# Three more odd up steps of two FFNs made as seven products, the first down tiles prepared in the last pair, and four smaller edits

## The chip, the cores and the metric

One core of a Trainium2 chip runs the whole program. The metric is the device time of one execution in microseconds (us). The engines are those of the profile: PE (TensorE matmul), PEld (its weight loads), DVE (VectorE), ACT (ScalarE), POOL (GpSimd), SP (SyncE, which here only issues transfers). A product of fp32 matrices is made in three passes of fp32r matmuls: each operand is split into a high half (a copy rounded to fp32r, made by ACT) and a low half (the rest, made by DVE), and high x high, low x high and high x low are added up in one PSUM bank.

## The reference, cut to what matters

A trunk of two layers on 512 tokens of width 1024. Layer 0 mixes by gated linear attention, layer 1 by a sparse attention (NSA) over keys and values shared from the state between the layers; both also attend to a memory. Behind each mixer comes the same kind of FFN, which is where most of the change lies:

```python
def conv_ffn(x, w_up, conv_w, conv_b, w_down):
    S = x.shape[1]
    u = x @ w_up                                  # 512 x 1024 @ 1024 x 5632
    u_pad = jnp.pad(u, ((0, 0), (CONV_WIDTH - 1, 0), (0, 0)))
    hc = conv_b
    for j in range(CONV_WIDTH):                   # width 3, along the tokens
        hc = hc + conv_w[j] * u_pad[:, j:j + S]
    a, b = split_cols(hc, (FFN_DIM, FFN_DIM))     # FFN_DIM 2816
    return (jax.nn.silu(a) * b) @ w_down          # 2816 x 1024

for i in range(2):
    ...
    h = h + concatenate([main, mem_attention]) @ w_out[i]
    h = h + conv_ffn(rmsnorm(h, norm_ffn[i]), w_up[i], conv_w[i], conv_b[i], w_down[i])
return rmsnorm(h, final_norm)
```

One edit lies in the compression of the shared keys and values (`silu(flat @ cmp_w1 + b1) @ cmp_w2 + b2`), right behind which layer 1 projects its queries.

## The kernel before

**The up steps.** The 2816 columns of a and of b are cut into NJ = 22 steps of 128; step j makes columns 128j to 128j+127 of a (half 0) and of b (half 1), features on the partitions and the 512 tokens along a row. A *plain* step (the loop at the end of `up`, L1268) is 2 x 24 matmuls of 512 columns: 8 slices of the 1024 input features, 3 passes each. `wget` loads a weight tile of 128 x 1024 on SP's queue and splits it. `gate` then makes silu(a) * b.

**Pairs.** For the odd steps listed in `FAST`, 9 to 19 in layer 0 and 7 to 19 in layer 1, the function `pairs` does an even step and the odd one behind it together. The even one is plain (`plain`, L1162, 48 matmuls of 512 columns). The odd one is a product of 2 x 2 blocks (a and b; first and last 512 input features; first and last 256 tokens) and is made by Strassen's scheme as seven products in place of eight (`product`, L1168): 7 x 4 slices x 3 passes = 84 matmuls of 256 columns. Products 1 to 3 use plain blocks of x, products 4 to 7 use sums of blocks of x. `forms` makes these sums in place of the rows x was made from and splits them: the high halves into one tile of tag "h" (the buffer of the residual h, which has been spilled to DRAM; a tile takes 128 x (V_N + 7 + 4096) floats), the low halves into scratch of the FFN. In the plain part of `up` two calls of `forms` stand behind steps fast[0]-3 and fast[0]-2, the third in the first pair.

Within `pairs`, `load` issues the next transfers four items ahead, `high` and `low` split a tile, `step` does the convolution, `close` and `finish` end the odd step's b in the pair behind it, and the order on ACT and DVE is that of the text (`Ordered`, whose recording line is L201, links each instruction to the one before while `on` is set). At the end of a pair it makes the next pair's first three weights (w0, w1, wa).

**Sums of weights.** The seven products also need sums of blocks of w_up (one block for each fast step) and of w_down (one for each p = 0..10, in both layers). They are formed ahead in DRAM, in the tensor qsum: two copies of 512 KB a block on SP's queue (`copy`, L280, 70 in all), then three accumulating transfers on POOL's queue, of 512, 256 and 256 KB (`pace`, L289, 105 in all; blocks go in groups of three, all first stages of a group ahead of its second). Calls of `copy` and `pace` are spread over the kernel, each behind an instruction that it follows.

**The down product.** It is made from seven products as well. Three of them (5, 7, 6) run inside the up stage: `mms(p, (6,))` and `mms(p, (5, 7))`, where `fill(j, half)` says so in a plain step, or at fixed places in a pair; `weights(p)` loads and splits their weights. Products 1 to 4 run behind the up stage, over tiles of w_down streamed in: `parts(s)` loads and splits tile s, `step(s)` uses it. So L1346 (layer 0, `ffn_features`) and L1535 (layer 1, `ffn_seven`) occur within the up stage and behind it. `back` reloads h from its spill, for the additions of the down product.

**The first query weight.** `project(0)` of layer 1 calls `wget` with a gain: POOL multiplies the raw tile by the gain of the norm (L350), then it is split (L353 ACT, L354 DVE). At that time DVE finishes the compression (`done`, L1982: hid, from which TensorE makes L1933).

In a span of 1222 us the stages lie so: input projections and attention of layer 0 to 208, w_out to 236, up 236 to 514, down to 580; layer 1's mixer 580 to 833, w_out to 872, up 872 to 1148, down and the last norm to 1214.

Of the kernel before, what the change touches and what calls it, by code (L numbers as in the profile page):

```python
# [24 lines left out]
FAST = ((9, 11, 13, 15, 17, 19), (7, 9, 11, 13, 15, 17, 19))  # L25
# [185 lines left out]
class Trunk:  # L211
# [113 lines left out]
    def wget(self, i, gain=None, ks=range(KC), halves=False):  # L325

        nc = self.nc
        raw = self.wload(i)
        if gain is not None and len(ks) <= 4:
            wh = self.t(self.wsp, [128, 1024], "wh", FR)  # L330
            wl = self.t(self.wsp, [128, 1024], "wl", FR)
            n = 1024 // len(ks)
            for r, k in enumerate(ks):
                o = slice(n * r, n * r + n)
                self.split_to(wh[:, o], wl[:, o], raw[:, o], self.gain(gain, k))
                if i == self.W["nsav"][3] and self.mem_scale:
                    self.after(self.high_ins, self.mem_scale)
            return wh, wl
        if gain is not None:
            a, n = V_GAIN + 8 * gain + ks[0], len(ks)  # L340
            g = self.vec[:, a:a + n].unsqueeze(2).to_broadcast([128, n, 1024 // n])
            v = raw.rearrange("p (k c) -> p k c", k=n)
            if halves:
                wh, wl = (self.t(self.wsp, [128, 1024], t, FR) for t in ("wh", "wl"))
                for r in range(2):
                    c, o = slice(n // 2 * r, n // 2 * r + n // 2), slice(512 * r, 512 * r + 512)
                    nc.gpsimd.tensor_tensor(out=v[:, c], in0=v[:, c], in1=g[:, c], op=ALU.mult)
                    self.split_to(wh[:, o], wl[:, o], raw[:, o])
                return wh, wl
            nc.gpsimd.tensor_tensor(out=v, in0=v, in1=g, op=ALU.mult)  # L350
        wh = self.t(self.wsp, [128, 1024], "wh", FR)
        wl = self.t(self.wsp, [128, 1024], "wl", FR)
        self.split_ins = nc.scalar.activation(wh, raw, AF.Copy)  # L353
        self.low_ins = nc.vector.tensor_tensor(out=wl, in0=raw, in1=wh.bitcast(F32), op=ALU.subtract)  # L354
        return wh, wl
# [278 lines left out]
    def gla_layer(self):  # L634
        nc, I, tc = self.nc, self.I, self.tc
        with ExitStack() as outer:
# [30 lines left out]
            with tc.tile_pool(name="glap", bufs=1) as pp:  # L667
# [42 lines left out]
                def queries_keys(i):  # L710
                    j, r = divmod(i, 2)
                    if i < 3:
                        qp = qps[i]
                    else:
                        qp = self.ps("sc" if i == 3 else "acc")
                        self.projA(qp, self.wget(self.W[("glak", "glaq")[r]][j]))
                        if i > 3:
                            self.copy(self.move)
# [73 lines left out]
            with tc.tile_pool(name="glac", bufs=2) as cp:  # L792
# [167 lines left out]
                for P in range(8):  # L960
# [12 lines left out]
                    self.pace(laid[0], 2)  # L973
# [96 lines left out]
    def up(self, l, pool, rows, us, fill, gate, pe, space=None, seven=None):  # L1070
# [12 lines left out]
        def forms(n):  # L1083
# [3 lines left out]
            def halves(q, raw, los):  # L1087
                n = (5, 7, 4, 6).index(q)
                hi = T["high"][:, 1024 * n:1024 * n + 1024].rearrange("p (k t) -> p k t", k=4)
# [25 lines left out]
        def pairs(js):  # L1115
# [8 lines left out]
            for j in js:  # L1124
                p, b = self.downb(l, j // 2 - 1), self.upb(l, j + 1)
                items += [(q(qs, p, 2),), (q(qs, b, 2), q(qs, b, 1)), (q(qd, b, 3), q(qs, b, 3)), (q(qs, p, 0, 2),), (q(qd, b, 0),),
                          (wp[up[2 * j + 4]],), (wp[up[2 * j + 5]],), (wp[up[2 * j + 6]],) if j == js[-1] else first(j + 2)]
# [42 lines left out]
            def step(j, half, u, dst, *parts):  # L1170
                self.conv(l, j, half, u, dst, parts)
                if "act" in parts:
                    self.pace(self.conv_ins, int(l or half or j % 2) + l * half * (j % 2))
                    if l == 0 and half:
                        self.copy(self.conv_ins)
# [17 lines left out]
            for j in js:  # L1193
# [36 lines left out]
                w0 = low(high())  # L1230
                w1 = high()
                dve.tensor_tensor(out=v2, in0=v2, in1=bass.AP(tensor=B.tensor, offset=B.offset + 256, ap=[B.ap[0], [-256, 2], [1, 256]]), op=ALU.subtract)
                w1 = low(w1)
# [3 lines left out]
                mms(p, (5, 7))  # L1237
# [3 lines left out]
                wa = high()  # L1241
                step(j + 1, 0, A, hc[0], "dve")
                act.activation(hc[0], hc[0], AF.Silu)
                wa = low(wa)
# [5 lines left out]
            ready.extend((w0, w1, wa))  # L1250
# [9 lines left out]
        for j in range(NJ):  # L1260
# [9 lines left out]
            if fast and fast[0] - 1 <= j <= fast[-1]:  # L1270
                if j in fast:
                    continue
                if j == fast[0] - 1:
                    pairs(range(j, fast[-1], 2))
                    if l == 0:
                        back(nc.gpsimd)
# [34 lines left out]
            self.pace(self.conv_ins, 3 if l else 1 + j % 2)  # L1311
            if l or j % 2:
                self.copy(self.conv_ins)
# [8 lines left out]
        if l:  # L1322
            back(nc.sync)

    def ffn_features(self, l):
# [42 lines left out]
        with ExitStack() as stack:  # L1368
# [54 lines left out]
            def fill(j, half):  # L1423
                p = j // 2 - 1
                if j == NJ - 1:
                    if half:
                        mms(p, (6,))
                        weights(T - 1)
# [15 lines left out]
            self.up(l, pool, rows, [us[:, half] for half in range(2)], fill, gate, pe, ap, (ops, mms))  # L1444
# [26 lines left out]
            parts(0)  # L1471
            parts(1)
# [42 lines left out]
    def ffn_seven(self, l):  # L1515
# [110 lines left out]
        def end(mms):  # L1626
# [8 lines left out]
            parts(0)  # L1635
            parts(1)
# [85 lines left out]
        with ExitStack() as stack:  # L1722
# [7 lines left out]
            with tc.tile_pool(name=f"up{l}", bufs=2) as pool:  # L1730
# [38 lines left out]
                def fill(j, half):  # L1769
                    p = j // 2 - 1  # L1770
                    if j == NJ - 1:
                        if half:
                            mms(p, (6,))
                            weights(T - 1)
# [17 lines left out]
                self.up(l, pool, rows, u, fill, gate, pe, ap, (ops, mms))  # L1792
# [21 lines left out]
    def nsa_layer(self):  # L1814
        nc, I, tc = self.nc, self.I, self.tc
        GKV, GMIX = 6, 1
        with ExitStack() as outer:
# [194 lines left out]
            def project(a):  # L2012

                wh, wl = self.wget(self.W["nsaq"][a], GMIX)
                if a > 1:
                    after(self.split_ins, self.mem_exp if a == 2 else turned[2 * a - 6])
                ps = self.ps("acc")
# [258 lines left out]
```

## Time and profile before

| | us |
|---|---|
| median of 3 runs (1224.05 to 1224.95) | 1224.61 |
| the profiled execution | 1224.07 |
| its span | 1222.3 |
| mean granted TensorE clock in it | 0.997 |

Busy time by stage, from the view of windows (stretch; its length and then the busy time and instructions of PE, PEld, DVE, ACT, POOL; granted clock, share of DMA, GB/s):

```profile
116.00:208.00 92.00, 92.00 (x897) 79.17 (x896) 72.06 (x226) 50.23 (x151) 33.58 (x60) 1.00 0.84 162
236.00:515.00 279.00, 278.91 (x1652) 248.32 (x1650) 229.24 (x342) 150.64 (x228) 28.82 (x36) 1.00 0.79 211
580.00:833.00 253.00, 249.76 (x1811) 213.53 (x1811) 187.32 (x456) 161.73 (x428) 99.33 (x115) 0.99 0.49 148
872.00:1148.00 276.00, 275.87 (x1502) 239.93 (x1501) 233.63 (x348) 150.44 (x213) 38.36 (x46) 1.00 0.85 204
1148.00:1214.00 66.00, 66.00 (x314) 54.86 (x313) 48.43 (x70) 35.63 (x57) 0.71 (x1) 1.00 0.46 148
```

The second and fourth row are the two up stages. PE is busy in nearly all of each, DVE for 229 of 279 us and 234 of 276. In the group views a row names line, engine, operation, output and inputs with their shapes and a count; a row of instructions begins with its start and its duration; rows in brackets say how long the engine was idle before and what ended that.

### The profile page before, as it was taken

How to read it: one execution, taken by the hardware profiler on the slowest of the kernel's cores; microseconds unless marked ns; L12 is line 12 of the kernel's file. 1: busy time of each engine (PE TensorE's matmuls, PEld its weight loads, DVE VectorE, ACT ScalarE, POOL GpSimd, SP SyncE). 2: the span in 40 equal slices, each digit the busy share in tenths (PEclk: the TensorE clock that was granted, in tenths of full speed). 3: DMA queues.
4: the chain of work that ended last, by engine and by line, in shares of the span. 5: the costliest groups of instructions: out<-in, count | busy, mean ns of one | idle time of the engine just before them, and what ended most of it. 6: DMA issues, size and time to landing. Idle time of an engine off the chain costs nothing.

```text
span 1222.3 us, 20705 instructions
## 1 busy us (share of the span) xinstructions
PE 1211.1 (99%) x7657; PEld 1052.1 (86%) x7657; DVE 950.4 (78%) x1723; ACT 694.0 (57%) x1321; POOL 220.8 (18%) x286
## 2 busy tenths in 40 slices
PE   9999999999999999999999999999999999999997
PEld 7888889888899999899888888888888889988886
DVE  7875887599678888778767577984699888888685
ACT  7656555456445555546534777783456455556454
POOL 1011342010010101100112155662021211110000
PEclk9999999999999999999999999999999999999999
DMA  8587699756779798887765334536799999985544
GB/s 294 187 224 198 143 173 173 272 155 170 181 204 229 212 224 228 254 260 223 213 197 168 84 110 143 180 120 156 235 177 187 242 209 212 216 230 172 173 128 147
DMA packets 88384, 235.47 MB, mean 193 GB/s; under 512 B 10111, under 2 KB 13984, under 8 KB 87772
## 3 DMA queue, kind: packets, MB, share of 16 engines
q1 hardware_dynamic: 71148, 192.61, 48.7%
q0 software_dynamic: 15328, 39.04, 22.4%
q10 hardware_dynamic: 1808, 2.51, 0.7%
q8 instruction: 60, 0.98, 0.3%
q14 instruction: 40, 0.33, 0.1%
HBM read 222.01 MB, written 79.74 MB: 247 GB/s over the span
## 4 chain that ended last, share of the span: by engine, by line
PE 95%; DVE 2%; issue 1%; DMA 1%; ACT 0%; SPq 0%; POOLq 0%; POOL 0%; ACTq 0%; DVEq 0%
PE acc L1268 14%; PE acc L1162 12%; PE acc L1168 11%; PE acc L1040 5%; PE acc L389 4%; PE acc L789 4%; PE po L2009 3%; PE po L407 3%; PE sc L1346 3%; PE po L1346 3%; PE acc L1346 3%; PE sc L1535 2%; PE po L1535 2%; PE acc L2009 2%; PE acc L407 2%; PE acc L1535 2%
## 5 line engine op out<-in xcount | busy, mean ns | idle before, releaser
L201 DVE TENSOR_TENSOR wl<-wraw,wh 128x1024 fp32r<-128x1024 f32 (+2 forms) x128 | 147.5, 1161 | 25.9 <-ACT wh L201 24.5
L201 ACT ACTIVATE wh<-wraw 128x1024 fp32r<-128x1024 f32 (+2 forms) x128 | 128.1, 1007 | 50.5 <-issue 14.8
L201 DVE SCALAR_TENSOR_TENSOR hc<-acc,taps,hc 128x511 f32<-128x511 f32 (+1 forms) x144 | 107.6, 748 | 46.6 <-ACT hc L201 44.2
L353 ACT ACTIVATE wh<-wraw 128x1024 fp32r<-128x1024 f32 x80 | 84.5, 1057 | 92.3 <-PE acc L1040 33.3
L289 POOL DMA_DIRECT2D qsum<-qsum x70 | 58.6, 901 | 336.0 <-ACT hc L201 226.0
L354 DVE TENSOR_TENSOR wl<-wraw,wh 128x1024 fp32r<-128x1024 f32 x80 | 101.4, 1267 | 19.4 <-ACT wh L353 18.7
L201 ACT ACTIVATE hc<-acc,taps 128x512 f32<-128x512 f32 x72 | 55.8, 775 | 90.2 <-DVE acc L201 38.5
L1268 PE MATMUL acc<-xh,wh 128*128 128x512 f32 x272 | 105.9, 390 | 0.1
L1268 PE MATMUL acc<-xh,wl 128*128 128x512 f32 x272 | 105.9, 389 | 0.0
L1268 PE MATMUL acc<-xl,wh 128*128 128x512 f32 x272 | 105.8, 389 | 0.0
L1162 PE MATMUL acc<-xl,wh 128*128 128x512 f32 x208 | 81.0, 389 | 0.0
L1162 PE MATMUL acc<-xh,wl 128*128 128x512 f32 x208 | 81.0, 389 | 0.0
L1162 PE MATMUL acc<-xh,wh 128*128 128x512 f32 x208 | 80.9, 389 | 0.0
L2075 POOL TENSOR_TENSOR P<-P,ssm 128x256 f32<-128x256 f32 (+3 forms) x48 | 64.8, 1372 | 1.9
L289 POOL DMA_DIRECT2D qsum<-in_qd x35 | 30.7, 928 | 166.8 <-ACT hc L201 106.5
L1268 PEld LDWEIGHTS acc<-xh,wh 128*128 128x128 f32 x272 | 51.1, 188 | 10.9 <-issue 0.5
L1268 PEld LDWEIGHTS acc<-xl,wh 128*128 128x128 f32 x272 | 51.1, 188 | 10.6
L1268 PEld LDWEIGHTS acc<-xh,wl 128*128 128x128 f32 x272 | 51.1, 188 | 10.3
L2067 ACT ACTIVATE P<-P,smn 128x128 f32<-128x128 f32 (+3 forms) x96 | 53.2, 557 | 11.4 <-DVE smn L2065 9.9
L1162 PEld LDWEIGHTS acc<-xl,wh 128*128 128x128 f32 x208 | 39.0, 188 | 8.2
L1162 PEld LDWEIGHTS acc<-xh,wl 128*128 128x128 f32 x208 | 39.0, 188 | 7.8
L1162 PEld LDWEIGHTS acc<-xh,wh 128*128 128x128 f32 x208 | 39.1, 188 | 7.7
(630 smaller groups left out, 3771.7 us busy)
## 6 DMA issues: line engine op xcount, KB each, us to landing
wraw<-in_wp SPq DMA_DIRECT2D x122, 512.0 KB, 4.8
qsum<-in_qd SPq DMA_DIRECT2D x70, 512.0 KB, 6.3
qsum<-in_qd POOLq DMA_DIRECT2D x35, 512.0 KB, 9.3
qsum<-qsum POOLq DMA_DIRECT2D x70, 256.0 KB, 7.2
wraw<-qsum SPq DMA_DIRECT2D x30, 512.0 KB, 5.1
wraw<-in_qd SPq DMA_DIRECT2D x30, 512.0 KB, 5.1
wraw<-qsum SPq DMA_DIRECT2D x51, 256.0 KB, 5.8
wraw<-in_qd SPq DMA_DIRECT2D x26, 256.0 KB, 5.0
```

Of the source, the lines that this page charges most:

```text
L201: ins = f(*a, **kw)
L289: ins = self.nc.gpsimd.dma_start(to, what, accum_op=ALU.add)
L353: self.split_ins = nc.scalar.activation(wh, raw, AF.Copy)
L354: self.low_ins = nc.vector.tensor_tensor(out=wl, in0=raw, in1=wh.bitcast(F32), op=ALU.subtract)
L407: self.move = nc.tensor.matmul(ps[:, :N], s_, m_, start=k == 0 and n == 0, stop=k == KC - 1 and n == 2)
L1040: self.move = nc.tensor.matmul(banks[m], a[:, o], b, start=k == 6 and i == 0, stop=k == 5 and i == 2)
L1162: pe(nc.tensor.matmul(dst, w[a][:, o], self.x[k][b], start=k + n == 0, stop=k == KC - 1 and n == 2))
L1168: pe(nc.tensor.matmul(dst, w[a][:, o], (X if n < 4 else T)[n][k][x], start=first and k + i == 0, stop=k == 3 and i == 2, skip_group_check= ...
L1268: pe(nc.tensor.matmul(pu[half], a[:, o], self.x[k][b], start=k == 0 and n == 0, stop=k == KC - 1 and n == 2))
L1346: pe(nc.tensor.matmul(dst, a[:, o], b, start=first and n == 0 and i % 2 == 0, stop=stop and n == 2, skip_group_check=True))
L1535: pe(nc.tensor.matmul(bank[i][:, c], a[:, ts], b[:, c], start=first and n == 0, stop=stop and n == 2, skip_group_check=True))
L2075: nc.gpsimd.tensor_tensor(out=P, in0=P, in1=f[:, i, :].unsqueeze(2).to_broadcast([128, 2, 128 * t + 128]), op=ALU.mult)
```

## The change

Six things change; what is computed stays the same up to rounding.

1. `FAST` becomes 7, 9, ..., 21 for both layers: eight pairs in each, 16 in place of 13. Layer 0 gains the pairs (6, 7) and (20, 21), layer 1 the pair (20, 21). So no plain steps follow the pairs, and `forms` stands behind steps 4 and 5 in layer 0. There are 38 blocks of sums (35), so 76 copies and 114 accumulating transfers.
2. In the last pair w0 and w1 are not the next pair's weights: in their places stand `ahead(0)` and `ahead(1)`, which are `parts(0)` and `parts(1)`, the first two streamed down tiles; wa is left out, and the last pair's items are not followed by loads of further up weights. The last pair's `mms(p, (5, 7))` moves behind its end, and `fill(NJ - 1, 1)`, now only `weights(T - 1)`, follows it. The two calls of `parts` at the start of the down stage go away.
3. `back` is issued on POOL's queue right behind the pairs in both layers; before, layer 1 issued it on SP's queue at the end of `up`.
4. In layer 0 the high halves of the sums of x start 24 floats (96 bytes) further on in their tile.
5. The multiply by the gain for the first query weight gets a dependency on `done`: it starts when hid is made.
6. Copies and sums are issued in other numbers: two copies at a time in `queries_keys`; 3 sums in place of 2 in the first four rounds of the chunk loop of layer 0; `2 + l` sums and one copy in each plain up step (before: 1 + j % 2 and a copy in odd ones in layer 0, 3 and one in layer 1); in a pair, one sum fewer in layer 1, and in layer 0 the copies behind both halves of the odd step.

```diff
-FAST = ((9, 11, 13, 15, 17, 19), (7, 9, 11, 13, 15, 17, 19))
+FAST = (tuple(range(7, NJ, 2)),) * 2
...
-            nc.gpsimd.tensor_tensor(out=v, in0=v, in1=g, op=ALU.mult)
+            self.gain_ins = nc.gpsimd.tensor_tensor(out=v, in0=v, in1=g, op=ALU.mult)
...
-                            self.copy(self.move)
+                            self.copy(self.move, 2)
...
-                    self.pace(laid[0], 2)
+                    self.pace(laid[0], 3 if P < 4 else 2)
...
-                n = (5, 7, 4, 6).index(q)
-                hi = T["high"][:, 1024 * n:1024 * n + 1024].rearrange("p (k t) -> p k t", k=4)
+                n = 1024 * (5, 7, 4, 6).index(q) + (0 if l else 24)
+                hi = T["high"][:, n:n + 1024].rearrange("p (k t) -> p k t", k=4)
...
-                          (wp[up[2 * j + 4]],), (wp[up[2 * j + 5]],), (wp[up[2 * j + 6]],) if j == js[-1] else first(j + 2)]
+                if j < js[-1]:
+                    items += [(wp[up[2 * j + 4]],), (wp[up[2 * j + 5]],), first(j + 2)]
...
-                    self.pace(self.conv_ins, int(l or half or j % 2) + l * half * (j % 2))
-                    if l == 0 and half:
+                    self.pace(self.conv_ins, int(l or half or j % 2))
+                    if l == 0 and j % 2:
                         self.copy(self.conv_ins)
...
-                w0 = low(high())
-                w1 = high()
+                if j < js[-1]:
+                    w0 = low(high())
+                    w1 = high()
+                else:
+                    ahead(0)
                 dve.tensor_tensor(out=v2, in0=v2, in1=bass.AP(tensor=B.tensor, offset=B.offset + 256, ap=[B.ap[0], [-256, 2], [1, 256]]), op=ALU.subtract)
-                w1 = low(w1)
+                if j < js[-1]:
+                    w1 = low(w1)
+                else:
+                    ahead(1)
...
-                mms(p, (5, 7))
+                if j < js[-1]:
+                    mms(p, (5, 7))
...
             act.on = dve.on = False
-            ready.extend((w0, w1, wa))
+            mms(p, (5, 7))
+            fill(NJ - 1, 1)
...
                     pairs(range(j, fast[-1], 2))
-                    if l == 0:
-                        back(nc.gpsimd)
+                    back(nc.gpsimd)
...
-            self.pace(self.conv_ins, 3 if l else 1 + j % 2)
-            if l or j % 2:
-                self.copy(self.conv_ins)
+            self.pace(self.conv_ins, 2 + l)
+            self.copy(self.conv_ins)
...
-        if l:
-            back(nc.sync)
...
                 if j == NJ - 1:
-                    if half:
-                        mms(p, (6,))
-                        weights(T - 1)
+                    weights(T - 1)
                     return
...
             banks[4], banks[3] = banks[7], banks[5]
-            parts(0)
-            parts(1)
...
+                if a == 0:
+                    tc.add_manual_dep(self.gain_ins.ins, done.ins.name, mybir.DependencyInfo(mybir.DependencyClass.Sync, mybir.DependencyReason.DATA), reason="order")
```

More of the change, by code (lines that the diff above doesn't have):

```diff
@@ L1068, in conv, with up @@
                 self.dve.scalar_tensor_tensor(out=dst[:, i:], in0=u[:, :S - i], scalar=tap(2 - i), in1=dst[:, i:], op0=ALU.mult, op1=ALU.add)
-    def up(self, l, pool, rows, us, fill, gate, pe, space=None, seven=None):
+    def up(self, l, pool, rows, us, fill, gate, pe, ahead, space=None, seven=None):
         nc = self.nc
@@ L1125, in pairs @@
                 p, b = self.downb(l, j // 2 - 1), self.upb(l, j + 1)
-                items += [(q(qs, p, 2),), (q(qs, b, 2), q(qs, b, 1)), (q(qd, b, 3), q(qs, b, 3)), (q(qs, p, 0, 2),), (q(qd, b, 0),),
-                          (wp[up[2 * j + 4]],), (wp[up[2 * j + 5]],), (wp[up[2 * j + 6]],) if j == js[-1] else first(j + 2)]
+                items += [(q(qs, p, 2),), (q(qs, b, 2), q(qs, b, 1)), (q(qd, b, 3), q(qs, b, 3)), (q(qs, p, 0, 2),), (q(qd, b, 0),)]
+                if j < js[-1]:
+                    items += [(wp[up[2 * j + 4]],), (wp[up[2 * j + 5]],), first(j + 2)]
             raws, count = [], [0]
@@ L1240, in pairs @@
                 step(j + 1, 0, A, hc[0], "act")
-                wa = high()
+                if j < js[-1]:
+                    wa = high()
                 step(j + 1, 0, A, hc[0], "dve")
                 act.activation(hc[0], hc[0], AF.Silu)
-                wa = low(wa)
+                if j < js[-1]:
+                    wa = low(wa)
                 product(4, B[:, E], wd[0], 0)
@@ L1443, in ffn_features @@
             even, toks = [], {}
-            self.up(l, pool, rows, [us[:, half] for half in range(2)], fill, gate, pe, ap, (ops, mms))
+            self.up(l, pool, rows, [us[:, half] for half in range(2)], fill, gate, pe, parts, ap, (ops, mms))
             hs = self.hs
@@ L1634, in end @@
             turns = [(0, 1), (1, 1), (2, 1), (3, 1), (2, 0), (3, 0), (0, 0), (1, 0)]
-            parts(0)
-            parts(1)
             for i in range(2):
@@ L1771, in fill @@
                     if j == NJ - 1:
-                        if half:
-                            mms(p, (6,))
-                            weights(T - 1)
+                        weights(T - 1)
                         return
@@ L1791, in ffn_seven @@
                 u = [us[:, half] for half in range(2)]
-                self.up(l, pool, rows, u, fill, gate, pe, ap, (ops, mms))
+                self.up(l, pool, rows, u, fill, gate, pe, parts, ap, (ops, mms))
                 end(mms)
```

## The prediction

> **What bounds the kernel now.** I read the page first: busy times (1), then the chain that ended last (4).
>
> ```profile
> PE 1211.1 (99%) x7657; PEld 1052.1 (86%) x7657; DVE 950.4 (78%) x1723; ACT 694.0 (57%) x1321; POOL 220.8 (18%) x286
> PE 95%; DVE 2%; issue 1%; DMA 1%; ACT 0%; SPq 0%; POOLq 0%; POOL 0%; ACTq 0%; DVEq 0%
> ```
>
> TensorE is busy for 1211 of the 1222 us of the span and carries 95% of the chain. So matmul time that is removed shortens the run, unless a new wait takes its place, and work that is added elsewhere costs nothing while it stays beside matmuls. The table of who waited for whom, TensorE alone, has two rows after the start of the program (us in total, times, longest):
>
> ```profile
> PE pt L1933 <- DVE hid L1982: 1.8, 1, 1.8
> PE pt L2010 <- ACT PT L2177: 1.3, 1, 1.3
> ```
>
> Then I read the chain in order of time (start, us, what) through the up stages of both layers.
>
> ```profile
> 305.35 16.35 PE acc L1268 x72
> 336.83 10.88 PE acc L1162 x48
> 349.11 8.62 PE acc L1168 x72
> 360.56 1.43 PE acc L1168 x12
> 361.99 10.89 PE acc L1162 x48
> ...
> 487.85 5.45 PE acc L1268 x24
> 493.40 5.72 PE acc L1268 x24
> 514.23 11.20 PE acc L1346 x96
> ...
> 1047.32 10.91 PE acc L1162 x48
> 1059.59 8.55 PE acc L1168 x72
> 1070.88 1.41 PE acc L1168 x12
> 1072.30 10.91 PE acc L1162 x48
> ...
> 1122.26 10.91 PE acc L1268 x48
> 1148.12 10.88 PE acc L1535 x48
> ```
>
> L1268 is the plain step, L1162 and L1168 are the pair: 48 matmuls of 512 columns, then 84 of 256. The rows left out are down products, and the pieces follow one another without idle time, so a stage is as long as its matmuls.
>
> **The change part by part.**
>
> *Three more pairs.* Step 6 of layer 0 begins when 24 of the 72 matmuls from 305.35 are done, at 305.35 + 24 x 0.227 = 310.80, and step 7 ends at 336.83: 26.03 us. One pair there takes 361.99 - 336.83 = 25.16. Saved: 0.87. Steps 20 and 21 of layer 0 take 514.23 - 487.85 = 26.38 (with 0.1 of idling and a slow start around 493.4): saved 1.22. In layer 1 they take 1148.12 - 1122.26 = 25.86 and a pair 1072.30 - 1047.32 = 24.98: saved 0.88. Both forms hold the same down products, so these differences contain all that TensorE does. Sum: **2.97 us**. It is little because 84 matmuls of 256 columns cost 8.62 + 1.43 = 10.05 us, not 7/8 of a plain step's 10.9.
>
> *High halves at another address.* The 84 small matmuls take 10.05 in layer 0 and 8.55 + 1.41 = 9.96 in layer 1, with the same shapes and order. The high halves lie at one address in both layers, while the scratch around the others is shifted by 224 bytes in layer 1. So places matter by about 0.09 us a pair. Moving the halves by 96 bytes in layer 0 could give it layer 1's rate, do nothing, or cost as much: bounds -0.7 to +0.7 us for 8 pairs. I take a gain of **0.7**, nearest to layer 1's row, which shows that the faster rate exists.
>
> *The gain of the first query weight waits.* DVE, POOL and TensorE around 642 us (start, us, engine, line, operation, operands), and the stretch from 644 to 648 (its third number from the end is the granted clock):
>
> ```profile
> 626.50 0.28 DVE L1982 SCALAR_TENSOR_TENSOR hid<-cth,chu 128x124 f32<-128x124 f32 x1
> 641.89 1.87 DVE L1982 SCALAR_TENSOR_TENSOR hid<-cth,chu 128x124 f32<-128x124 f32 x1
> 641.64 1.98 POOL L350 TENSOR_TENSOR wraw<-wraw,h 128x1024 f32<-128x1024 f32 x1 [2.48 <-DMA wraw<-in_wp]
> 643.91 0.42 PE L1933 MATMUL pt<-cw,hid 128*32 128x64 f32 x8 [1.82 <-DVE hid L1982]
> 644.26 0.39 PE L389 MATMUL acc<-ml,wh 128*128 128x256 f32 x1
> 648.13 0.28 PE L407 MATMUL po<-wh,mh 128*128 128x256 f32 x1
> 644.00:648.00 4.00, 4.00 (x27) 3.91 (x27) 3.88 (x12) 1.03 (x3) 0.11 (x1) 0.59 0.38 124
> ```
>
> The same instruction took 0.28 us alone and 1.87 beside POOL's multiply, and TensorE waited 1.82 for it. Held back until it is done, the multiply no longer meets it: 1.87 - 0.28 = **1.6 us**. Second, behind that gap the granted clock is 0.59: the 19 matmuls of 256 columns from 644.26 to 648.13 take 3.87 us, against 0.12 each, 2.3 us, at the pace of the rows at 349 and 360. With a gap of about 0.5 us I expect no drop: the wait of 1.3 us on L2010 lies in a stretch whose clock is full,
>
> ```profile
> 660.00:830.00 170.00, 168.58 (x1332) 143.39 (x1331) 130.88 (x355) 123.34 (x351) 88.56 (x100) 1.00 0.42 122
> ```
>
> so another **1.6 us**. The price: the multiply now starts 0.5 us later, ends near 644.2, and meets the low half of a value weight on DVE, an operation with two operands in SBUF like the stretched one.
>
> ```profile
> 644.02 1.21 DVE L354 TENSOR_TENSOR wl<-wraw,wh 128x1024 fp32r<-128x1024 f32 x1
> 664.59 5.44 PE acc L2009 x24
> ```
>
> If that one has to wait, it ends near 645.4, where it ends now (645.2). The weight that the multiply makes is used at 664.6, or 661.4 after the gain, still 17 us behind it. On POOL nothing that TensorE needs soon stands behind the wait. Nothing is charged. Bounds: 0 (the wait moves on) and 3.2; I take 3.2, as 0.28 is measured.
>
> The Trainium skill, "TensorE: Matmul & The Clock Gate", part 1, says that the clock falls to half after a window of about 3.4 us of idling. By that rule a gap of 2.1 us need not be the cause, and the drop would stay. The trace has the 0.59 right behind the gap, which speaks against it.
>
> *Layer 0's pairs start two steps earlier.* `forms` moves from steps 6 and 7 to 4 and 5, where DVE has no idle time to speak of. But it runs there already: its operations do not depend on steps 6 and 7 and are scheduled ahead,
>
> ```profile
> 295.31 1.21 DVE L201 TENSOR_TENSOR rows<-rows,rows 128x1024 f32<-128x1024 f32 x1
> ```
>
> before step 5 begins. Charge 0; without that cover, the 1.2 us of one such operation or two. Layer 1 starts its pairs at step 6 already.
>
> *The last pair and what follows.* Its two next weights become the first two down tiles: the same two splits of 1024 columns at the same places; a third is dropped. The reload of h moves to POOL in layer 1, where nothing is queued behind it until the ending. In both layers h is wanted 16 blocks of 12 small matmuls later (2 + 11 + 3, at 1.4 us: 22 us) and lands in 10.4:
>
> ```profile
> h<-spill POOLq DMA_DIRECT2D x1, 2048.0 KB, 10.4
> qsum<-in_qd POOLq DMA_DIRECT2D x35, 512.0 KB, 9.3
> qsum<-qsum POOLq DMA_DIRECT2D x70, 256.0 KB, 7.2
> half<-qsum SPq DMA_DIRECT2D x13, 256.0 KB, 6.5
> 30.00:40.00 10.00, 10.00 (x42) 7.40 (x41) 9.87 (x18) 7.47 (x15) 0.00 (x0) 1.00 0.19 55
> ```
>
> What stood behind the pairs, two plain steps, also gave DVE time; see the third rival.
>
> *More copies and sums.* Three more blocks bring 6 copies on SP and 9 accumulating transfers on POOL. Counted from the code, 26 sums are issued before layer 0's up stage (22 now), 62 before its end (55), 85 before layer 1's pairs (78). The two extra copies in the first projections fall where DMA is busy 0.19 (last row). Four extra sums go into the chunk loop, one in each of four rounds:
>
> ```profile
> 133.66 1.68 POOL L289 DMA_DIRECT2D qsum<-qsum  x2 [1.46 <-PE po L789]
> 136.03 0.19 POOL L913 TENSOR_SCALAR oss<-oss 128x2 f32<-128x2 f32 x1 [0.69 <-ACT C L878]
> ```
>
> One sum takes 0.84 of POOL and the idle 0.69 hides most of it; the norm on DVE comes 0.2 us later or a little more, and TensorE has gate matmuls to go on with: 0, at most 0.5.
>
> **Sum:** 2.97 + 0.7 + 1.6 + 1.6 = 6.9 us. The profiled execution took 1224.07 (its span and 1.8 around it): 1217.2. The median of the runs shown lies 0.54 above that execution, so I predict **1217.7**.
>
> **Rivals.**
> 1. *The half clock stays.* Only the wait goes: 1217.7 + 1.6 = 1219.3. For it: the rule cited above. Against: the place of the 0.59. Chance 0.12.
> 2. *The address goes the wrong way:* 1217.7 + 1.4 = 1219.1. Chance 0.07.
> 3. *DVE is late behind the last pair.* In a middle pair product 4 ends at 1072.30, and two operations on DVE read
>
> ```profile
> 1073.14 0.68 DVE L201 TENSOR_TENSOR sq<-half,sq 128x512 fp32r<-128x512 f32 x1
> 1079.27 0.42 DVE L201 TENSOR_TENSOR a12l<-hc,a12h 128x256 fp32r<-128x256 f32 x1
> ```
>
> The second is the gate's last: it ends 7.4 us behind the product. The last down weights (3 x 0.68) and the third down tile (1.2) make 10.6; TensorE has 6 blocks, 8.4 us, before it needs that tile. So 2.2 to 2.4 us are lost at each end if nothing is done ahead: 1220.1 with one, 1222.5 with both. Against: these splits are not tied to the pair's order, and DVE is idle 22% of the time (first row). Chance 0.05 for one, 0.10 for both.
>
> 4. *Slower: the last sums come late.* In layer 1 a pair now issues 4 sums and uses 6. The second stage of the last pair's down block becomes the second sum of the pair before, and the first load of the last pair waits for it. The middle pair shows the place of that sum on POOL and of ScalarE's use of the load:
>
> ```profile
> 1084.74 0.84 POOL L289 DMA_DIRECT2D qsum<-qsum  x1 [1.59 <-ACT hc L201]
> 1096.61 0.62 ACT L201 ACTIVATE sq<-half 128x512 fp32r<-128x512 f32 x1
> ```
>
> That is 12.4 and 24.3 us into the pair. With the landings quoted above the load is there at 12.4 + 7.2 + 6.5 = 26.1, 1.8 late, and the bank that the next plain half needs 5.45 us into the last pair comes free 1.8 later too, about when it is wanted: up to 1 us lost. If the landings doubled under the added traffic, the first stage (issued about 2) lands at 21, the second at 35, the load at 42: 17 us late, some 15 of them TensorE's: 1217.7 + 15 = 1233. Slower than before from about 8 us of delay. Against: today no load of a pair makes TensorE wait. Chance 0.09.
>
> **How the numbers follow.** The forecast has 0.57. Alone it reaches from 1216.0 (the 1.3 us wait on L2010 may go as all shifts by 3 us, and the address may give a little more) to 1219.0 (no gain by the address, 0.5 in the chunk loop). One late end, the half clock with such losses, or 3 us at the last load reach 1221.5. Range 1216.0 to 1221.5; it leaves out both ends late and doubled landings. A measurement of this kernel can tell about 0.2% (2.4 us) from no change. Faster: 0.57 + 0.12 + 0.07 + 0.05 = 0.81; same: 0.10; slower: 0.09.
>
> **What would show it.** Right: 16 pairs of about 25.0 us (25.16 in layer 0 if the address does nothing), no plain steps behind them; L1982 at 0.28 both times, no wait of TensorE for it and a full clock behind it; h landed before the first addition into it. Wrong: a wait of TensorE of over 1 us behind a last pair, a wait on a sum ahead of layer 1's last pair, a longer chunk loop in layer 0, or a clock still low where L1933 stands.

## The result and the profile after

The changed kernel takes 1232.07 us (median of 5 runs, 1228.64 to 1232.49), the kernel before 1224.05 beside it (5 runs, 1221.94 to 1224.95): ratio 1.0061, 95% interval 1.0042 to 1.0079. It is slower by some 7.5 us; the forecast was 1217.7 and its range ended at 1221.5. In experiments below a ratio is always to the kernel before on the same chip. The profiled execution took 1232.07, too.

The page of the changed kernel: its first line, the busy times, and the chain that ended last, by engine.

```profile
span 1230.3 us, 21015 instructions
PE 1207.7 (98%) x7765; PEld 1053.2 (86%) x7765; DVE 962.2 (78%) x1741; ACT 700.2 (57%) x1330; POOL 227.5 (18%) x296
PE 88%; DVE 5%; DMA 3%; ACT 2%; issue 1%; POOL 0%; SPq 0%; POOLq 0%; ACTq 0%; DVEq 0%
```

TensorE's own work did shrink, by 3.4 us (1211.1 to 1207.7), and the span grew by 8.0. So the loss is time in which TensorE waits: its share of the chain fell from 95% to 88%, and DVE, transfers and ACT hold 10% of it, 3% before. The view of who waited for whom, TensorE alone (us in total, times, longest), names them; before the change it had two rows behind the program's start, both in the prediction.

```profile
PE acc L1353 <- DVE hc L201: 3.4, 2, 2.1
PE pt L790 <- DVE v L918: 2.6, 1, 2.6
PE acc L1538 <- ACT wh L201: 2.2, 1, 2.2
PE po L789 <- ACT v L907: 1.7, 1, 1.7
PE acc L1538 <- DVE hc L201: 1.4, 1, 1.4
...
```

Lines of the changed kernel are shifted: L1353 and L1538 are the down products of the two layers, L1279 is the plain step, L1163 and L1169 are the pair, L789 and L790 lie in the chunk loop of layer 0. To see in which stage the time was lost, I take from the chain of waits the first piece of each stage: the first up step and the first matmul of layer 1's mixer, then the first up step and the first pair of layer 1. Before:

```profile
235.63 5.44 PE acc L1268 x24
580.15 0.70 PE acc L1868 x3
872.11 5.44 PE acc L1268 x24
947.42 10.88 PE acc L1162 x48
```

And after:

```profile
239.55 5.44 PE acc L1279 x24
585.57 0.70 PE acc L1867 x3
874.13 5.44 PE acc L1279 x24
951.58 10.88 PE acc L1163 x48
```

Differences of these starts, and of the spans for the last row:

| stage | before | after | change | forecast |
|---|---|---|---|---|
| up to the first up step of layer 0 (the chunk loop is in it) | 235.63 | 239.55 | +3.92 | 0 |
| FFN of layer 0 | 344.52 | 346.02 | +1.50 | -2.8 |
| mixer and w_out of layer 1 | 291.96 | 288.56 | -3.40 | -3.2 |
| plain up steps of layer 1 | 75.31 | 77.45 | +2.14 | 0 |
| pairs of layer 1 to the end | 274.88 | 278.72 | +3.84 | -0.9 |

One row is as forecast. Four places cost what was booked at nothing: the chunk loop, the plain steps of layer 1, and the end of each up stage. (From its first matmul to the start of w_out the chunk loop takes 96.15 us, 91.47 before: 4.7 more. What comes ahead of it was 0.8 shorter in this execution, so the first row shows 3.9.)

**The chunk loop.** POOL in the changed kernel (start, us, engine, line, operation, operands; in brackets the idle time before it and what ended that). L913 and L914 make the factor of the norm.

```profile
151.91 0.88 POOL L289 DMA_DIRECT2D qsum<-qsum  x1 [1.22 <-PE po L789]
156.71 0.81 POOL L289 DMA_DIRECT2D qsum<-qsum  x1 [3.92 <-DMA qsum<-in_qd]
158.75 0.82 POOL L289 DMA_DIRECT2D qsum<-qsum  x1 [1.23 <-DMA qsum<-qsum]
159.64 0.19 POOL L913 TENSOR_SCALAR oss<-oss 128x2 f32<-128x2 f32 x1
```

The same factor in the kernel before, where no sum ahead of it waited for a landing:

```profile
154.98 1.62 POOL L913 TENSOR_SCALAR oss<-oss 128x2 f32<-128x2 f32 x1 [0.55 <-ACT jk L909]
```

The second sum of the changed kernel's rows adds to a block whose first stage is still on its way. POOL stands still for 3.92 us until it has landed, and again 1.23 for the third; behind them waits the factor, which in the kernel before began at 154.98. In the last rounds a sum holds POOL for another 4.18 us. The Trainium skill, "TensorE: Matmul & The Clock Gate", part 1, "Architectural detail", calls the queues of ScalarE and VectorE strict first in, first out, and GpSimd's too, for each of its cores; these rows of POOL agree.

**The ends of the up stages.** ACT behind the last pair of layer 0, and below it the load on SP's queue for which it waits.

```profile
508.76 1.06 ACT L201 ACTIVATE wh<-wraw 128x1024 fp32r<-128x1024 f32 x1
...
513.50 1.06 ACT L201 ACTIVATE wh<-wraw 128x1024 fp32r<-128x1024 f32 x1 [2.48 <-DMA wraw<-in_qd]
514.47 0.76 ACT L201 ACTIVATE hc<-acc,taps 128x512 f32<-128x512 f32 x1
```

```profile
508.73 3.41 SPq L1358 DMA_DIRECT2D wraw<-in_qd  x3
```

The first row is the second streamed down tile (`ahead(1)`), prepared in good time. The second is the *third* tile, `parts(2)`, which the pair's order doesn't link. The compiler's order put it ahead of the odd step's convolution (last row); its load could only leave at 508.73, when a buffer came free, and ACT waited 2.48 us for it. The convolution reads PSUM bank A, and the bank's release is what the down products wait for (the rows with hc above): two banks of tag "acc" hold the last pair's a and b, and the first streamed product needs the same two. In layer 1 the same row waits 2.79 us. (There the first wait, 2.2 us, is put down to another split on ACT, which ended at 1153.55; DVE's last read of the bank ended at 1153.46, so both were late by about as much.)

**The plain steps of layer 1.** On SP's queue, before (weights follow at 895.88) and after (two views):

```profile
895.44 0.32 SPq L1142 DMA_DIRECT2D more<-qsum  x1
```

```profile
899.19 0.32 SPq L1143 DMA_DIRECT2D more<-qsum  x1
899.62 1.72 SPq L322 DMA_DIRECT2D wraw<-in_wp  x3
```

The first row of each is a load for the first pair, which needs a finished sum and stands in the queue ahead of weights of the plain steps. Counted from the first up step it leaves 23.33 us in before the change and 25.06 after. The sum it needs is the 62nd before, the second of three issued from 886.92 on; after the change it is the 70th, the third of three from 888.95 on. ACT then waits for the weights:

```profile
905.96 1.06 ACT L353 ACTIVATE wh<-wraw 128x1024 fp32r<-128x1024 f32 x1 [6.31 <-DMA wraw<-in_wp]
```

Before, that split waited for its load, too, but began 29.66 us behind the first up step; here it is 31.83.

```profile
901.77 1.07 ACT L353 ACTIVATE wh<-wraw 128x1024 fp32r<-128x1024 f32 x1 [4.15 <-DMA wraw<-in_wp]
```

**What came out as forecast.** The second hid row on DVE (the first, at 631.92, takes 0.28), a weight's low half that the multiply now meets, and the stretch from 644 to 648 (third number from the end: the granted clock):

```profile
647.17 0.29 DVE L1981 SCALAR_TENSOR_TENSOR hid<-cth,chu 128x124 f32<-128x124 f32 x1
647.71 2.86 DVE L354 TENSOR_TENSOR wl<-wraw,wh 128x1024 fp32r<-128x1024 f32 x1
644.00:648.00 4.00, 3.90 (x39) 3.63 (x37) 3.87 (x7) 3.92 (x9) 0.85 (x2) 1.00 0.39 131
```

The stretch of hid is gone, so is the wait of 1.82, and the clock is full. The stretch moved to the low half, as the prediction allowed: 2.86 us beside the multiply, 1.21 before. TensorE does not wait for it.

### The profile page after: what moved, and what is told of

The parts are those of the page before. It is cut to its first block, busy times and chain, and to the rows that moved or that the text cites. A ratio compares the mean times of both kernels' runs of the same rounds, so it can differ in the third digit from the quotient of the medians.

```text
span 1230.3 us, 21015 instructions
## 1 busy us (share of the span) xinstructions
PE 1207.7 (98%) x7765; PEld 1053.2 (86%) x7765; DVE 962.2 (78%) x1741; ACT 700.2 (57%) x1330; POOL 227.5 (18%) x296
## 4 chain that ended last, share of the span: by engine, by line
PE 88%; DVE 5%; DMA 3%; ACT 2%; issue 1%; POOL 0%; SPq 0%; POOLq 0%; ACTq 0%; DVEq 0%
PE acc L1163 14%; PE acc L1169 12%; PE acc L1279 7%; PE acc L1040 5%; PE acc L389 4%; PE po L2008 3%; PE po L407 3%; PE acc L789 2%; PE sc L1353 2%; PE po L1353 2%; PE acc L1353 2%; PE acc L2008 2%; PE acc L407 2%; PE sc L1538 2%; PE po L1538 2%; PE acc L1538 2%
## 5 line engine op out<-in xcount | busy, mean ns | idle before, releaser
L201 DVE TENSOR_TENSOR wl<-wraw,wh 128x1024 fp32r<-128x1024 f32 (+2 forms) x135 | 156.0, 1164 | 27.6 <-ACT wh L201 25.5
L1163 PE MATMUL acc<-xl,wh 128*128 128x512 f32 x256 | 99.7, 389 | 0.0
L1163 PE MATMUL acc<-xh,wl 128*128 128x512 f32 x256 | 99.7, 389 | 0.0
L1163 PE MATMUL acc<-xh,wh 128*128 128x512 f32 x256 | 99.7, 389 | 0.0
L1279 PE MATMUL acc<-xh,wh 128*128 128x512 f32 x176 | 68.6, 390 | 0.3 <-DVE us L1318 0.3
L1279 PE MATMUL acc<-xh,wl 128*128 128x512 f32 x176 | 68.5, 389 | 0.0
L1279 PE MATMUL acc<-xl,wh 128*128 128x512 f32 x176 | 68.5, 389 | 0.0
L1163 PEld LDWEIGHTS acc<-xl,wh 128*128 128x128 f32 x256 | 48.1, 188 | 10.1
L1163 PEld LDWEIGHTS acc<-xh,wl 128*128 128x128 f32 x256 | 48.1, 188 | 9.6
L1163 PEld LDWEIGHTS acc<-xh,wh 128*128 128x128 f32 x256 | 48.1, 188 | 9.5
L1169 PE MATMUL acc<-xl,wh 128*128 128x256 f32 x192 | 54.4, 283 | 0.0
L1169 PE MATMUL acc<-xh,wl 128*128 128x256 f32 x192 | 54.3, 283 | 0.0
L1169 PE MATMUL acc<-xh,wh 128*128 128x256 f32 x192 | 54.3, 283 | 0.0
```

The lines of the kernel that those rows point to most:

```text
L201: ins = f(*a, **kw)
L1163: pe(nc.tensor.matmul(dst, w[a][:, o], self.x[k][b], start=k + n == 0, stop=k == KC - 1 and n == 2))
L1169: pe(nc.tensor.matmul(dst, w[a][:, o], (X if n < 4 else T)[n][k][x], start=first and k + i == 0, stop=k == 3 and i == 2, skip_group_check= ...
L1279: pe(nc.tensor.matmul(pu[half], a[:, o], self.x[k][b], start=k == 0 and n == 0, stop=k == KC - 1 and n == 2))
```

## The experiments

Theories: **A**, the third tile's split holds the convolution at both ends; **B**, sums hold POOL in the chunk loop; **C**, a load that waits for a sum holds SP's queue in layer 1. All are edits of the changed kernel unless the text says "kernel before".

### e5: the gain edit alone, on the kernel before

```diff
-            nc.gpsimd.tensor_tensor(out=v, in0=v, in1=g, op=ALU.mult)
+            self.gain_ins = nc.gpsimd.tensor_tensor(out=v, in0=v, in1=g, op=ALU.mult)
...
+                if a == 0:
+                    tc.add_manual_dep(self.gain_ins.ins, done.ins.name, mybir.DependencyInfo(mybir.DependencyClass.Sync, mybir.DependencyReason.DATA), reason="order")
```

> The kernel before, with only the multiply by the gain held until hid is made. The forecast's two terms (the stretch of hid and the half clock behind the gap): 3.2 us shorter than the kernel before, from the mixer of layer 1 alone. Rival 1 of the prediction (the half clock stays): 1.6 us shorter. Rival (the multiply only meets another operation): no change.

1220.84 us (6 runs, 1220.23 to 1222.49), ratio 0.9975 (0.9964 to 0.9987): 3.1 us shorter. What is left of the wait:

```profile
PE pt L1933 <- DVE hid L1982: 0.2, 1, 0.2
```

Both terms of the forecast are there, and rival 1 (the half clock stays) is out for this place.

### e1: the third tile's split behind the last convolution (A)

```diff
             self.split_to(wh, wl, w)
+            if s in (2, 3):
+                self.after(self.high_ins, self.conv_ins)
```

(and the same in `ffn_seven`.)

> The changed kernel, with the split of the third and fourth streamed down tile tied behind the last convolution on ScalarE. Theory A (at both ends of the up stages the third tile's split stands ahead of the odd step's convolution in ScalarE's order and waits 2.5 and 2.8 us for its load, so PSUM banks come free late): the TensorE waits of 3.4 and 3.6 us at the two ends go, the execution is 7 to 7.5 us shorter than the changed kernel. Rival (VectorE's load behind the last pair is too much in any order, as rival 3 of the prediction had it): the waits stay within 1 us of what they are, the time changes by under 2 us.

1225.13 us (10 runs, 1224.15 to 1228.86), ratio 1.0016 (1.0005 to 1.0028): about 5.5 us shorter than the changed kernel by the two ratios, less than the 7 to 7.5 expected. The FFN of layer 0 is 2.4 shorter than in the changed kernel and the last stage 2.7. The waits at the ends:

```profile
PE acc L1540 <- DVE hc L201: 1.1, 1, 1.1
PE acc L1353 <- DVE hc L201: 1.0, 1, 1.0
```

They fall from 3.4 and 3.6 to 1.0 and 1.1. The wait for the first bank is gone; for the second some of it stays, since other splits still lie on DVE between the two banks' last reads.

### e3: two sums a round in the chunk loop (B, inconclusive)

```diff
-                    self.pace(laid[0], 3 if P < 4 else 2)
+                    self.pace(laid[0], 2)
...
-                self.pace(self.move if l else self.low_ins)
+                self.pace(self.move if l else self.low_ins, 1 + (m < (0 if l else 4)))
```

> The changed kernel, with two sums a round in the chunk loop of layer 0 as before, and the four sums taken from there issued in w_out of layer 0. Theory B (the third sum of a round brings sums against the landing of the sums that they build on, POOL is held, and the norm behind it is late): the waits of POOL on DMA (8.1 us) and the waits of TensorE in the chunk loop (4.3 us) go, w_out of layer 0 starts near 208.2 in place of 212.2; 3.9 us shorter. Rival (the loop is longer for the extra copies and the traffic, not for the sums): it starts at 211 or later, the time is as that of the changed kernel within 1 us.

1241.22 us (4 runs), ratio 1.0135 (1.0118 to 1.0151). The edit does less than it says: w_out of layer 0 issues sums only at its steps 3 and 4, so one sum is moved there and three come later all the way. The last two leave at 1160 and 1166 us, behind the loads of layer 1's last pair, so that layer multiplies by unfinished sums. TensorE waits 10.4 us at the end of layer 0's up stage, where a load on SP waits 16.4 for its sum, and 5.1 at that of layer 1. This is the mechanism of rival 4, in a kernel that really is short of sums. The chunk loop itself got better: w_out starts at 210.30, against 212.32.

### e4: three more sums before layer 1's up stage (C)

```diff
-                self.pace(self.move if l else self.low_ins)
+                self.pace(self.move if l else self.low_ins, 1 + (m < (3 if l else 0)))
```

> The changed kernel, with three more sums issued in w_out of layer 1, so that the 70th sum leaves before that layer's up stage. Theory C (on SP's queue a load for the first pair, which needs the 70th sum, stands ahead of weights of the plain steps; it is held until 899.2, and the weights land late): the load leaves SP before 885, ScalarE's wait of 6.3 us for the weights goes, the plain steps of layer 1 lose 2 us less. Rival (the plain steps are late for VectorE's work, which forms and the gates fill): the 2.1 us stay.

1229.33 us (4 runs, 1228.65 to 1230.83), ratio 1.0043 (1.0028 to 1.0058), which by itself can't be told from 1.0061. The stage shows more: the load for the first pair has left SP before 869, the weights leave from 881.44 on, and the split that waited 6.31 us for its load waits for TensorE alone.

```profile
881.44 17.04 SPq L322 DMA_DIRECT2D wraw<-in_wp  x4
902.27 1.07 ACT L353 ACTIVATE wh<-wraw 128x1024 fp32r<-128x1024 f32 x1 [3.15 <-PE acc L1279]
```

From the first up step's first matmul (873.00) to the first pair's (948.31) it is 75.31 us, as in the kernel before (871.95 to 947.26); in the changed kernel it is 77.45 (873.97 to 951.42). C holds by these rows. Its size varies: with this stage's code as in the changed kernel, e1, e6, e6b, e9 and e11 lose 1.0, 0.9, 0.7, 0.3 and 0.9. With the code of the kernel before, e5 gains 0.4 and e12 loses 0.7, so not all of the 2.1 need be the load's.

### e8 and e11: three sums a round, in another order (B)

e8 puts more room between a sum and the one that it builds on, by larger groups of blocks:

```diff
-        self.jobs = [(b, n) for i in range(0, len(blocks), 3) for n in range(3) for b in blocks[i:i + 3]]
+        GROUPS = [(0, 6), (6, 4), (10, 3), (13, 3), (16, 2)] + [(i, 3) for i in range(18, 38, 3)]
+        self.jobs = [(b, n) for i, k in GROUPS for n in range(3) for b in blocks[i:i + k]]
```

> The changed kernel with three sums a round as it has them, but with the first ten blocks in groups of six and four, so that a sum and the one that it builds on are two rounds apart. If POOL is held for the landing of the sum before (theory B): its waits on DMA in the chunk loop (8.1 us) fall under 2 us and w_out of layer 0 starts at 208 to 209.5. If the third sum's own time on POOL or its traffic is the cost: it starts at 211 or later.

1236.54 us (2 runs), ratio 1.0112 (1.0094 to 1.0131); w_out starts at 218.38. POOL no longer waits for a sum to land, but stands for 8.8 us where the profile shows no releaser ("issue"). Larger groups use more copies before they use sums, so a wait for copies would fit; the trace doesn't say so, and I leave it open.

e11 orders each round's sums behind the factor of the round before, and the last round's behind the last factor:

```diff
-                    self.pace(laid[0], 3 if P < 4 else 2)
+                    if nxt:
+                        self.pace(laid[0], 3 if P < 4 else 2, factor)
...
                         finish()
+                        self.pace(laid[0], 2, factor)
```

(`pace` gives each sum an order dependency on `factor[0]`, the last L914.)

> The changed kernel with its three sums a round, but each round's sums ordered on POOL behind the norm factor of the round before, and the last round's two behind the last factor. Theory B: no sum stands between the two operations of a factor or ahead of the last, so the TensorE waits on the norm go and w_out of layer 0 starts at 208 to 209.7, with as many sums in the loop as the changed kernel has. If the sums' number or traffic is the cost: 211 or later.

1235.41 us (4 runs), ratio 1.0102 (1.0087 to 1.0118); w_out starts at 215.97. The expectation fell:

```profile
201.70 0.91 POOL L289 DMA_DIRECT2D qsum<-qsum  x1 [11.35 <-DMA qsum<-qsum]
```

A sum behind one factor is still ahead of the next. Pushed back behind the factor that ended at 190.4, it came close upon the sum that it builds on and held POOL for 11.35 us, with the last factor (from 202.68) behind it. So neither of the two orders tried (e8, e11) helps within the loop.

### e12: three sums a round alone, on the kernel before (B)

```diff
-                    self.pace(laid[0], 2)
+                    self.pace(laid[0], 3 if P < 4 else 2)
```

> The kernel before with this one edit of the change: three sums in place of two in the first four rounds of the chunk loop. Theory B: the loop alone gets 2 to 5 us longer (it varies with when transfers land), the rest stays. If the loop is late only together with the added copies: no change.

1232.42 us (2 runs), ratio 1.0071 (1.0052 to 1.0091). w_out starts at 213.77, against 208.40; 5.2 us of that lie in the loop, with none of the other edits and without the extra copies. This one line costs 8.7 us by the ratio, more than the 6.9 that the forecast has as gains. Most of the rest lies in the FFN of layer 0, 4.9 us in the profiled execution (241.00 to 590.45, against 235.63 to 580.15):

```profile
PE acc L1346 <- DVE hc L201: 3.2, 1, 3.2
```

This is the same kind of wait for a bank at the end of that up stage, and ACT shows the same cause: a split of a down tile that waits for its load ahead of the convolution.

```profile
518.50 1.06 ACT L201 ACTIVATE wh<-wraw 128x1024 fp32r<-128x1024 f32 x1 [4.37 <-DMA wraw<-in_qd]
```

In the kernel before, the split in that place waited 1.70 us and was done 2 us before the convolution could begin. Here the two plain steps stand at the end, and the wait comes all the same. Why the load is later stays open.

### e7, e9 and e10: the costs taken away together

e7 takes all three away: `pace(laid[0], 2)`, three sums at steps 3 and 4 of w_out of layer 0, e4's edit, and e1's with the low halves tied behind the convolution on DVE as well.

> The changed kernel with all three costs taken away: two sums a round in the chunk loop and the four sums in w_out of layer 0, three sums earlier in w_out of layer 1, and the third and fourth streamed tile tied behind the last convolution on ScalarE and VectorE. If the three theories are right and add up: 12 to 14 us shorter than the changed kernel, 4 to 7 us (0.4 to 0.55%) shorter than the kernel before, about what the prediction had named, and shorter than the kernel before with the gain edit alone by 1.5 to 3 us. If a cost only moves: within 2 us of the kernel before.

1232.93 us (5 runs, 1231.0 to 1233.9), ratio 1.0086 (1.0072 to 1.01): some 10 us longer than the kernel before, which neither expectation has. The end of layer 1 was mended (no wait there of 0.2 us or more), but two costs had moved. First, w_out's sums followed a split of weights that is made early, so they came to stand in the chunk loop:

```profile
202.95 0.84 POOL L289 DMA_DIRECT2D qsum<-qsum  x1 [5.37 <-DMA qsum<-in_qd]
205.60:211.00 5.40, 5.40 (x28) 5.40 (x29) 2.58 (x7) 1.25 (x3) 0.00 (x0) 0.57 0.72 125
```

The last factor follows at 203.86. TensorE waited 7.2 us, and ran at a clock of 0.57 behind it. Second, in layer 0 the fourth tile's split now stood ahead of the last gate's on ACT: TensorE waited 2.6 us in L1353 for sh, which that gate makes.

e9 mends the first: two sums a round, and w_out's sums follow a matmul of w_out.

```diff
-                    self.pace(laid[0], 3 if P < 4 else 2)
+                    self.pace(laid[0], 2)
...
-                self.pace(self.move if l else self.low_ins)
+                self.pace(self.move, 1 if l else 3)
```

> The changed kernel with two sums a round in the chunk loop, and the four others in w_out of layer 0, where all sums now follow a matmul of w_out in place of an early split, so that none can stand ahead of the last norm factor on POOL. Theory B as widened by the two runs before (any sum that stands in POOL's order ahead of the norm's factor and waits for a copy or a sum to land holds the norm, whatever it was issued for): the loop loses under 1.5 us against the kernel before, w_out of layer 0 starts at 208 to 209.7. Rival (the loop is late for the traffic of the extra copies): 211 or later.

1226.83 us (8 runs, 1225.39 to 1228.83), ratio 1.0031 (1.0021 to 1.0041). w_out starts at 208.14 and the loop takes 91.54 us, with as many copies as the changed kernel: the traffic of the copies is not the cost. The waits at the ends are left (3.0 and 3.4 us). Over all runs the loop reads so (POOL: waits of its sums on a landing or without a shown releaser, as long as a factor still stands behind them; TensorE: its waits for L907 and L918; loop: from its first matmul to the start of w_out; all in us):

| kernel | POOL | TensorE | loop | w_out starts |
|---|---|---|---|---|
| before | 0.6 | 0 | 91.47 | 208.40 |
| e5 | 0.3 | 0 | 91.43 | 208.38 |
| e9 | 1.6 | 0 | 91.54 | 208.14 |
| e10 | 0.7 | 0 | 91.46 | 208.42 |
| e6b | 7.1 | 0.7 | 92.22 | 209.14 |
| e3 | 3.6 | 1.1 | 92.80 | 210.30 |
| e4 | 8.6 | 2.0 | 93.83 | 211.39 |
| e6 | 8.6 | 2.2 | 94.08 | 210.73 |
| after | 10.4 | 4.3 | 96.15 | 212.32 |
| e12 | 8.8 | 2.9 | 96.68 | 213.77 |
| e1 | 10.1 | 4.4 | 97.73 | 215.05 |
| e11 | 17.2 | 5.4 | 98.64 | 215.97 |
| e7 | 8.7 | 7.2 | 100.80 | 217.90 |
| e8 | 8.8 | 6.2 | 101.27 | 218.38 |

The loops of after, e1, e4, e6 and e6b are the same code: 0.7 to 4.4 us of waiting in one execution each, as the landings fall. The loop is longer by the wait of TensorE and, in some, by a clock under 1 behind it (e1 and e7: 0.59 and 0.57).

e10 adds to e9 the edit of e4 and both ends: the third tile's split behind the last convolution, the fourth's behind the last gate, on ACT and on DVE.

```diff
+            if s in (2, 3):
+                self.after(self.high_ins, self.conv_ins if s == 2 else self.act.last)
+                self.after(self.low_half, self.conv_dve if s == 2 else self.dve.last)
...
-                self.pace(self.move, 1 if l else 3)
+                self.pace(self.move, (1 + (m < 3)) if l else 3)
```

> The run before with three sums earlier in w_out of layer 1 and both ends tied: the third tile's split behind the last convolution, the fourth's behind the last gate, on ScalarE and VectorE. If all three theories are right: TensorE waits under 1 us at each end, the plain steps of layer 1 as before the change, 0.4 to 0.6% (5 to 7 us) shorter than the kernel before. If the ends only move their wait again: a wait of 2 us or more at one end and within 3 us of the kernel before.

1219.02 us (5 runs, 1218.75 to 1219.4), ratio 0.9962 (0.9949 to 0.9974): 4.7 us shorter than the kernel before, and shorter than either kernel of the case, though just under the 5 to 7 expected. All of TensorE's waits but the one for the program's first tile:

```profile
PE pt L2015 <- ACT PT L2184: 1.3, 1, 1.3
...
PE po L691 <- ACT xh L201: 0.9, 1, 0.9
PE acc L1353 <- DVE wl L201: 0.4, 1, 0.4
PE acc L1541 <- DVE wl L201: 0.2, 1, 0.2
```

e5, with the gain alone, stands at 0.9975; the three more pairs with the rest are worth the 0.0013 between them, 1.6 us, with intervals that overlap.

### e6 and e6b: the address of the high halves

Layer 0's offset 0 (as before) and 56 floats in place of 24:

```diff
-                n = 1024 * (5, 7, 4, 6).index(q) + (0 if l else 24)
+                n = 1024 * (5, 7, 4, 6).index(q) + 0
```

> The changed kernel with the high halves of layer 0 at their old address. If the address is what changed the pitch of the 84 small matmuls of a pair: 10.045 us a pair in layer 0, as in the kernel before, against 10.005 in the changed kernel; if something else did: 10.005.

> The changed kernel with the high halves of layer 0 moved by 56 floats (224 bytes, as far as the scratch of layer 1 is moved) in place of 24. If only the distance between high and low halves counts: 10.045 us or more a pair, as no distance is then layer 1's; if the place of each by itself counts, another sum than 10.005 and 10.045 is likely, by up to 0.08.

The 84 small matmuls of one pair of layer 0 in the chain, for e6 and the changed kernel:

```profile
375.77 8.62 PE acc L1169 x72
387.22 1.43 PE acc L1169 x12
```

```profile
377.30 8.56 PE acc L1169 x72
388.69 1.44 PE acc L1169 x12
```

10.05 and 10.00 us; e6b has 8.58 and 1.42, 10.00 as well. The address does it, by 0.05 a pair, and 224 bytes do as much as 96. All pairs of layer 0 that the chain shows whole have these lengths to 0.01; those of layer 1 stay at 9.96. (One run each: 1229.18 and 1226.12 us. Of the 3.1 between them the chunk loop has 1.9, by the table above, and layer 1's mixer 0.9: there e6 waits 1.0 for hid.)

## Why the prediction was wrong, step by step

- *What bounds the kernel:* right. Every matmul saved or wait added on TensorE shows in the span.
- *The gain waits* (3.2): right in size and mechanism, 3.4 in the stage and 3.1 alone. The multiply met the low half of a weight and stretched it to 2.86 us, and TensorE did not need that one soon. It is not safe in every execution: in e6, with the same edit, TensorE waited 1.0 us for hid, as four operations ahead of it on DVE took 4.21 us, 3.36 in the changed kernel.
- *Three more pairs* (2.97): the pairs are as long as forecast (339.86 to 365.00 in layer 0, 25.14 us), but a new wait came up where the two plain steps had stood at the end (below). In e10, with the ends mended, the FFN of layer 0 is 1.44 shorter of the 2.8 forecast with the address, and layer 1's last stage 0.2 longer in place of 0.9 shorter. So even then 1.2 us of the 3.7 forecast for pairs and address come home; waits of 0.6 at the two ends are part of the rest, and what else is stays open.
- *The address* (0.7): right in sign, too large. The place of the halves matters, by 0.05 for each of 8 pairs, 0.4, and not by the 0.09 of layer 1.
- *More copies and sums* ("0, at most 0.5"): **wrong, by 3.9 here** (4.7 in the loop itself). I priced the time that a sum takes on POOL (0.84) and its cover, but not that a sum holds POOL until the one that it builds on has landed. With three a round, one round, about 10 us (142.12 to 151.91 on POOL), lies between the stages of a group, and landings of 9.3 and 7.2 us were quoted in the prediction itself.
- *The last pair and what follows* ("the same two splits ... at the same places"): **wrong, by 4.3 and 4.7** (the FFN of layer 0 and the last stage against their forecasts; 0.3 of the first is the address). The step looked at the two tiles that are done ahead, not at the third, which is not linked and may stand anywhere. Rival 3 had the place (DVE late behind the last pair, 2.2 to 2.4 an end, 0.15 in all); its mechanism was another, since e1 takes 7.0 us of waits down to 2.1 without taking work away from DVE.
- *Rival 4, late sums:* its place was wrong in the changed kernel (no wait ahead of the last pair), and its mechanism, a load that waits for a sum on SP's queue, was at work elsewhere: in layer 1's plain steps, which took 2.1 us more. I had counted where sums are issued, not what stands behind a load that waits for one.

Sum of the misses: 3.9 + 4.3 + 4.7 + 2.1 - 0.2 (the gain) = 14.8, which is the way from 6.9 us gained to 8.0 lost in the profiled executions, within rounding.

## What to carry to other kernels

A transfer that waits for data held its whole queue here, on SP (the weights behind 899.19) as on POOL (3.92 us and up to 11.35): before more of them are issued, list for each what it waits for, when that lands, and what the engine has to do next for somebody else. Instructions that are not linked may be put ahead of linked ones; where work is prepared ahead, tie the piece that comes after it as well. And when the end of a stage is replaced, ask what will wait there: two plain ends made into pairs save 2.1 us of matmuls by the forecast, and 7.0 us of waits came up there; 0.6 are left in e10, where the order is tied.

## What the runs showed of the hardware

The half clock behind an idle stretch is not a matter of its length alone. Behind the wait of 1.8 us for hid the clock was 0.59 in the kernel before; behind the same wait in e12 it was full (first row). In the changed kernel a wait of 2.6 us in the chunk loop left it full (second), in e1 one of 1.9 at the same place did not (third).

```profile
654.30:658.00 3.70, 3.70 (x36) 3.61 (x37) 3.58 (x12) 1.90 (x3) 0.12 (x1) 1.00 0.40 122
198.50:202.50 4.00, 4.00 (x35) 3.99 (x36) 3.69 (x10) 1.67 (x4) 2.03 (x3) 1.00 0.77 114
199.80:204.00 4.20, 4.20 (x24) 4.20 (x24) 3.46 (x9) 1.67 (x4) 1.10 (x3) 0.59 0.86 92
```

The Trainium skill, "TensorE: Matmul & The Clock Gate", part 1, says that the window which the gate looks at runs freely, without regard to the kernel; that fits a drop that comes at one time and not at another. But these gaps are shorter than its window of about 3.4 us, by which none of the drops need have come; the measured 0.59 decides. The prediction weighed the drop by the gap's length alone.
